# A two-layer hybrid decoder on one Trainium2 core: top-k masks of four blocks as a TensorE product, and two reorderings of conversions

## The chip, the core and the metric

The kernel runs on one core of a Trainium2 chip. Five engines work side by side, each through its own queue in order: TensorE (PE, matrix products), VectorE (DVE), ScalarE (ACT), GpSimd (POOL) and SyncE (SP), which here issues nearly all DMA transfers. An instruction waits until the instructions that it needs on other engines have signalled; everything behind it on its own engine waits with it. The metric is the device time of one launch in microseconds.

## The reference, cut to what matters

The input is one sequence of 1024 tokens of width 1024, in float32. Layer 0 runs sliding-window attention and a state-space branch (S5) with a gated linear unit side by side; layer 1 is sparse attention: an indexer scores all earlier keys for every query, the best 256 are kept, and softmax attention runs over those.

```python
# layer 0, end of the S5 branch
y = jax.nn.gelu(y.reshape(bsz, L, W))
h = y @ glu_w + glu_b
return h[..., :W] * jax.nn.sigmoid(h[..., W:])

# layer 0: both branches side by side, then one projection
return jnp.concatenate([att, ssm], axis=-1) @ w_out

# layer 1, for one block of 128 queries
rel = jax.nn.relu(jnp.einsum('bqhd,bsd->bqhs', qi_blk, ki).astype(jnp.float32) * (IDX_DIM ** -0.5))
score = jnp.einsum('bqhs,bqh->bqs', rel, w_blk.astype(jnp.float32))
score = jnp.where(key_pos[None, None, :] <= t[None, :, None], score, NEG_INF)
_, idx = lax.top_k(score, topk)
...
logits = jnp.einsum('bqhgd,bqkhd->bqhgk', q_blk, k_sel).astype(jnp.float32) * (Dh ** -0.5)
...
logits = jnp.where(valid[:, :, None, None, :], logits + bias, NEG_INF)
p = jax.nn.softmax(logits, axis=-1).astype(v.dtype)
return jnp.einsum('bqhgk,bqkhd->bqhgd', p, v_sel)
```

## The kernel before

Products run in fp32r with each operand split into a high part (rounded) and a low part (the rest), so that each product is three matmuls: high by high, high by low, low by high. A weight chunk comes as `wraw` by DMA; ACT rounds it to `whi` (L153), and DVE or POOL forms `wlo = wraw - whi` (L154). Chunks are numbered in the order of their use; the list `LO_ON_V` (L126) names those whose low part DVE makes, all others go to POOL. Chunks 22 and 23 hold query weights of layer 1, chunk 24 the keys'. A low part is made in four instructions of 128x512.

The order of each engine's instructions comes from a scheduler that follows data dependencies and priorities, except for PE in most stages, where the code writes it out by hand. `behind(insts)` (L128) is a hint of order to that scheduler: what is issued inside it comes after the given instructions.

The linear unit (L852 to L889) runs over two weight chunks `i`, two halves of the tokens and two column groups `n2`, eight rounds in all. In each round PE makes two accumulators of 12 matmuls (L872 to L874); ACT takes a tanh of one (L879), DVE multiplies by the gate (L880) and by the other accumulator (L881), which frees it, and ACT and DVE split the result into high and low (L882, L883), the second half of the tile `cat`. The first half of `cat` is the attention branch: eight loads `at` (L887, four buffers) whose high part ACT makes (L888) and low part DVE (L889). Behind this come the output projections of layer 0, which add the input `xh`, loaded by SP (L903), to PE's product (L911).

In layer 1 the index scores (L1064 to L1072) alternate PE products `psi`, ACT's `relu` (three buffers) and DVE's weighted sum `sc`, while PE also runs the projections of queries, keys and values, whose rows are normalised by way of POOL's `nr` (L199, L200) and ACT's `st` (L392) and then transposed (L1151). The top-k threshold of each block is found by counting in a search: on DVE for blocks 7, 5 and 3 (L1221, which writes a scratch tile `vjunk` beside its counts), on ACT for the others. Ahead of it `flip` (L1198, L1199) turns scores into ordered integers, and after it `tie_mask` (L1282) uses `flip` again and leaves a mask `mk[b]` in bf16 that is zero for a kept key and a large number for another (L1302). Blocks 0 and 1 keep every earlier key; for them `mk0` masks the diagonal block alone.

`dsa_scores` (L1350) does the attention scores of one block and one key head, for four query heads: SP loads the bias tile `bt` (`st` for the first two units), POOL puts the mask on it (L1372 or L1374), PE makes the three score matmuls into `pq` (L1375 to L1377), DVE adds `pq` and `bt` and takes the row's extreme `mn` (L1379), ACT takes the exponential (L1385), and the rows are normalised, on ACT for two heads and on DVE for two (L1390). `dsa_tr` transposes the result on PE (L1401) and splits it (L1404 on ACT, `pT_lo` L1405 on DVE), and `dsa_out` multiplies by the values (L1415 to L1417). The query tile is split by ACT (`q1T_hi`, L1336) and POOL (`q1T_lo`, L1337). The units run blocks 0 to 3 of one key head, blocks 0 to 3 of the other, then blocks 4 to 7; the first two units are scored early, among gate projections, before the masks of the later blocks are ready.

## Time and profile before

| | us |
|---|---|
| median of 3 runs | 1068.32 |
| lowest and highest run | 1062.63, 1068.51 |
| the profiled execution | 1065.89 |
| its span | 1064.2 |

| engine | busy us | share of the span |
|---|---|---|
| PE | 1013.1 | 95% |
| DVE | 748.7 | 70% |
| ACT | 622.3 | 58% |
| POOL | 436.5 | 41% |

The mean granted clock of PE in the profiled execution was 0.987 of full speed. Busy shares are means over stages with different limits; a wait is told by the instruction that waited and the one that came last among those it waited for. In a row of a timeline the last bracket is the idle time ahead of the instruction and what ended it; "x4" means four of the same kind in a row.

### The profile page before, as it was taken

Reading aid. Unit: us, or ns where it says so; the run is one execution under the profiler, and the core shown is the slowest. Engines: PE = TensorE matmul, PEld = TensorE weight load, DVE = VectorE, ACT = ScalarE, POOL = GpSimd, SP = SyncE. Lnnn points to the kernel's source line nnn. Section 1 sums busy time; section 2 is a strip of 40 time slices with the busy share of each in tenths; the row PEclk is TensorE's granted clock in tenths of the full one; section 3 lists DMA queues with packets and bytes.
Section 4 is the critical chain, followed back from the end, with each engine's and each line's share of the span. In section 5 each row is a group of like instructions: output and inputs, shape, how many; then the busy total and the mean of one; then the engine's idle time right before and its main releaser. Section 6 shows DMA issues by size and latency. Waiting matters only on the chain.

```text
span 1064.2 us, 19143 instructions
## 1 busy us (share of the span) xinstructions
PE 1013.1 (95%) x6536; PEld 890.5 (84%) x6536; DVE 748.7 (70%) x1705; ACT 622.3 (58%) x1671; POOL 436.5 (41%) x722
## 2 busy tenths in 40 slices
PE   7899999999998999999999989999998889999998
PEld 5798999999864588877789989999886669898898
DVE  6628889973796554544667578888877986777742
ACT  7543653222787433434566989789967865565620
POOL 5897632221000002122041678678545847456000
PEclk9999999999999999999999999999999989999999
DMA  7282455339462317531020232122436644665333
GB/s 267 95 284 80 105 163 163 107 105 276 133 198 60 100 60 267 207 119 61 1 89 21 75 98 68 41 68 86 121 112 212 204 123 142 201 190 162 117 100 119
DMA packets 103697, 138.33 MB, mean 130 GB/s; under 512 B 9352, under 2 KB 79880, under 8 KB 98736
## 3 DMA queue, kind: packets, MB, share of 16 engines
q1 hardware_dynamic: 103600, 137.12, 41.3%
q8 instruction: 51, 0.84, 0.3%
q14 instruction: 46, 0.38, 0.1%
HBM read 102.31 MB, written 36.21 MB: 130 GB/s over the span
## 4 chain that ended last, share of the span: by engine, by line
PE 68%; DVE 14%; POOL 6%; ACT 5%; DMA 3%; issue 3%; SPq 1%; ACTq 0%; POOLq 0%; DVEq 0%
PE mm L234 8%; PE mm L232 8%; PE mm L233 8%; PE mm L218 5%; PE mm L219 5%; PE mm L220 5%; PE mm L1551 3%; PE mm L1552 3%; PE mm L1550 3%; PE psx L801 2%; PE tr L1401 2%; PE mm L1416 1%; PE mm L1417 1%; PE pq L1375 1%; PE tr L795 1%
## 5 line engine op out<-in xcount | busy, mean ns | idle before, releaser
L153 ACT CAST whi<-wraw 128x512 fp32r<-128x512 f32 (+1 forms) x152 | 87.3, 643 | 74.4 <-PE mm L233 38.2
L154 POOL TENSOR_TENSOR wlo<-wraw,whi 128x512 fp32r<-128x512 f32 x64 | 87.3, 1391 | 96.3 <-ACT whi L153 96.3
L219 PE MATMUL mm<-wlo,h1T_hi 128*128 128x256 f32 x384 | 110.3, 288 | 0.0
L218 PE MATMUL mm<-whi,h1T_hi 128*128 128x256 f32 x384 | 109.8, 288 | 0.2 <-DVE gst L981 0.2
L220 PE MATMUL mm<-whi,h1T_lo 128*128 128x256 f32 x384 | 109.6, 287 | 0.0
L1374 POOL TENSOR_TENSOR bt<-bt,mk 128x384 f32<-128x384 f32 (+3 forms) x80 | 82.5, 1049 | 61.9 <-DMA bt<-g_d 43.9
L919 POOL TENSOR_TENSOR acc<-acc,sq 128x512 f32<-128x512 f32 x12 | 18.1, 1507 | 195.4 <-DVE wlo L154 154.0
L1221 DVE TENSOR_SCALAR_CACHE_REDUCE vjunk<-sc,vt 128x512 bf16<-128x512 uint16 (+5 forms) x90 | 91.0, 1012 | 2.7
L232 PE MATMUL mm<-hT_hi,whi 128*128 128x256 f32 (+1 forms) x288 | 85.6, 297 | 0.0
L234 PE MATMUL mm<-hT_hi,wlo 128*128 128x256 f32 (+1 forms) x288 | 85.6, 297 | 0.0
L233 PE MATMUL mm<-hT_lo,whi 128*128 128x256 f32 (+1 forms) x288 | 85.5, 297 | 0.0
L1257 ACT ACTIVATE sjunk<-sc,st 128x384 bf16<-128x384 uint16 (+5 forms) x90 | 77.7, 864 | 6.2 <-POOL st L1261 4.2
L1550 PE MATMUL mm<-aT_hi,whi 128*128 128x256 f32 x256 | 73.5, 287 | 1.2 <-ACT aT_hi L1524 1.2
L218 PEld LDWEIGHTS mm<-whi,h1T_hi 128*128 128x128 f32 x384 | 72.9, 191 | 1.0 <-PE psi L1065 0.6
L219 PEld LDWEIGHTS mm<-wlo,h1T_hi 128*128 128x128 f32 x384 | 73.2, 191 | 0.4
L154 DVE TENSOR_TENSOR wlo<-wraw,whi 128x512 fp32r<-128x512 f32 (+1 forms) x88 | 62.9, 760 | 15.1 <-ACT whi L153 12.7
L1551 PE MATMUL mm<-aT_lo,whi 128*128 128x256 f32 x256 | 72.7, 284 | 0.7 <-DVE aT_lo L1525 0.7
L220 PEld LDWEIGHTS mm<-whi,h1T_lo 128*128 128x128 f32 x384 | 72.9, 190 | 0.4
L1552 PE MATMUL mm<-aT_hi,wlo 128*128 128x256 f32 x256 | 72.6, 284 | 0.0
L1385 ACT ACTIVATE s<-s,mn 128x384 f32<-128x384 f32 (+7 forms) x56 | 46.0, 821 | 30.9 <-DVE mn L1379 30.9
L1072 DVE SCALAR_TENSOR_TENSOR sc<-relu,wi,sc 128x384 f32<-128x384 f32 (+3 forms) x70 | 49.6, 711 | 20.3 <-ACT relu L1067 16.6
L392 ACT ACTIVATE st<-mm,nr 128x64 f32<-128x64 f32 (+1 forms) x160 | 46.0, 360 | 30.1 <-POOL nr L200 29.9
(398 smaller groups left out, 3478.7 us busy)
## 6 DMA issues: line engine op xcount, KB each, us to landing
wraw<-in_w_dram SPq DMA_DIRECT2D x20, 1024.0 KB, 5.0
wraw<-in_wo_dram SPq DMA_DIRECT2D x16, 1024.0 KB, 5.2
bt<-g_d SPq DMA_DIRECT2D x24, 256.0 KB, 4.6
g_d<-g1r_d SPq DMA_DIRECT2D x8, 576.0 KB, 10.8
bt<-g_d SPq DMA_DIRECT2D x24, 192.0 KB, 3.4
qT_d<-gst SPq DMA_DIRECT2D x32, 128.0 KB, 1.9
qT<-qT_d SPq DMA_DIRECT2D x32, 128.0 KB, 3.9
xh<-in_xT_dram SPq DMA_DIRECT2D x16, 256.0 KB, 5.7
```

The costliest lines, as they stand in the source:

```text
L153: S.copy(hi[p_], raw[p_])
L154: eng.tensor_sub(lo[p_], raw[p_], rd(hi[p_]))
L218: T.matmul(ps, a, hi[:, k, c0:c1], start=(k == 0), stop=False)
L219: T.matmul(ps, a, lo[:, k, c0:c1], start=False, stop=False)
L220: T.matmul(ps, b, hi[:, k, c0:c1], start=False, stop=(k == 7))
L232: T.matmul(o, a, hT[0][:, k, ts], start=(k == 0), stop=False)
L233: T.matmul(o, a, hT[1][:, k, ts], start=False, stop=False)
L234: T.matmul(o, b, hT[0][:, k, ts], start=False, stop=(k == 7))
L1221: V.tensor_scalar(junk[:, :128 * (b + 1)], data(b), self.thr(j), None, op0=OP.is_ge, op1=OP.add, accum_out=self.cnt[:, it, j:j + 1])
L1550: T.matmul(ps, a, aT[0][:, k, toks], start=(k == 0), stop=False)
L1551: T.matmul(ps, a, aT[1][:, k, toks], start=False, stop=False)
L1552: T.matmul(ps, b, aT[0][:, k, toks], start=False, stop=(k == 7))
```

## The change

It has three parts. The linear unit's attention conversions are put behind the last products of a half: those of the first half behind the round that ends chunk 0, those of the second half behind the last round. The low parts of chunks 22 and 23 go from POOL to DVE. And for blocks 0 to 3 POOL no longer puts the mask on the bias tile; PE adds it to the scores itself, as a first bf16 matmul with minus the identity (`nid`) and `mk[b]`, which for blocks 0 and 1 is now a bf16 tile of 256 columns (`mk01`). To make room in SBUF the search's scratch tile `vjunk` shares the memory of `flip`.

```diff
@@ -123,7 +123,7 @@
 
     wcount = [0]
     raw_pools = [wp]
-    LO_ON_V = (0, 1, 2) + tuple(range(9, 21)) + (29, 30) + tuple(range(33, 39))
+    LO_ON_V = (0, 1, 2) + tuple(range(9, 21)) + (22, 23) + (29, 30) + tuple(range(33, 39))
 
     def behind(insts):
 
@@ -853,6 +853,7 @@
         ca = tuple(cps[1 - half].tile([128, 8, 512], F32R, name=f"cat_{n}") for n in ("hi", "lo"))
         cat.append(ca)
     gbt = yp.tile([128, 4, L], F32, name="gbt")
+    glu_last = []
     for n in range(4):
         dma(gbt[:, n], gb_d[n])
     for i in range(2):
@@ -879,14 +880,18 @@
                 S.activation(sg, pp[0], AF.Tanh, scale=0.5, bias=glub[:, 1, 4 + n:5 + n])
                 V.scalar_tensor_tensor(sg, sg, 1.0, gt_, op0=OP.add, op1=OP.mult)
                 V.scalar_tensor_tensor(sg, pp[1], glub[:, 0, n:n + 1], sg, op0=OP.add, op1=OP.mult)
-                S.activation(ca[0][:, 4 + n], sg, AF.Copy, scale=0.25)
-                V.scalar_tensor_tensor(ca[1][:, 4 + n], sg, 0.25, rd(ca[0][:, 4 + n]), op0=OP.mult, op1=OP.subtract)
+                glu_hi = S.activation(ca[0][:, 4 + n], sg, AF.Copy, scale=0.25)
+                glu_lo = V.scalar_tensor_tensor(ca[1][:, 4 + n], sg, 0.25, rd(ca[0][:, 4 + n]), op0=OP.mult,
+                                                op1=OP.subtract)
+            glu_last.append((glu_hi.ins, glu_lo.ins))
     for half in range(2):
         for g in range(4):
             at = st3.tile([128, 512], F32, name="at", bufs=4)
             dma(at, att_d[g, :, half * 512:(half + 1) * 512])
-            S.copy(cat[half][0][:, g], at)
-            V.tensor_sub(cat[half][1][:, g], at, rd(cat[half][0][:, g]))
+
+            with behind(glu_last[1 + 2 * half]):
+                S.copy(cat[half][0][:, g], at)
+                V.tensor_sub(cat[half][1][:, g], at, rd(cat[half][0][:, g]))
     es_y.close()
     es_3.close()
     es_h1 = ExitStack()
@@ -1217,7 +1222,7 @@
             if it % 16 == 0:
                 self.t = self.start()
             for j, b in enumerate(self.blocks):
-                junk = tk.tile([128, L], BF16, name="vjunk")
+                junk = tk.tile([128, L], I32, name="flip").bitcast(BF16)
                 V.tensor_scalar(junk[:, :128 * (b + 1)], data(b), self.thr(j), None, op0=OP.is_ge, op1=OP.add,
                                 accum_out=self.cnt[:, it, j:j + 1])
             i = it % 16
@@ -1317,11 +1322,15 @@
     if "sc7" in dbg:
         dma(dbg["sc7"], sc[7])
 
-    mk0 = mp.tile([128, 128], F32, name="mk0")
+
+    mk01 = mp.tile([128, 256], BF16, name="mk01")
     with tc.issue_after(ki_lo.ins):
-        G.memset(mk0, 0.0)
-    G.affine_select(out=mk0, in_=mk0, pattern=[[-1, 128]], compare_op=OP.is_ge, fill=NEG,
+        G.memset(mk01, 0.0)
+    G.affine_select(out=mk01[:, 128:], in_=mk01[:, 128:], pattern=[[-1, 128]], compare_op=OP.is_ge, fill=FAR,
                     base=0, channel_multiplier=1)
+    mk[0], mk[1] = mk01[:, 128:], mk01
+    nid = mp.tile([128, 128], BF16, name="nid")
+    V.tensor_scalar(nid, ident, -1.0, None, op0=OP.mult)
 
     def dsa_q_load(b, kv):
         qr = akv.tile([128, 4, 128], F32, name="q1r", bufs=2)
@@ -1367,12 +1376,12 @@
                     bp_ = fp if b < 4 and nbt[0] > 6 and nbt[0] % 2 else pool_
                     bt = bp_.tile([128, 512], F32, name="bt", bufs=6)[:, :n]
                 last_ttr[1] = dma(bt, skewed(h, 1023 - 128 * b + c0, n)).ins
-                with behind(last_rstd):
-                    if b < 2:
-                        G.tensor_add(bt[:, w - 128:], bt[:, w - 128:], mk0)
-                    else:
+                if b < 4:
+                    T.matmul(o, nid, mk[b][:, ks], start=True, stop=False)
+                else:
+                    with behind(last_rstd):
                         G.tensor_sub(bt, bt, mk[b][:, ks])
-                T.matmul(o, qT[0][:, g], kT[0][:, kv, ks], start=True, stop=False)
+                T.matmul(o, qT[0][:, g], kT[0][:, kv, ks], start=b > 3, stop=False)
                 T.matmul(o, qT[0][:, g], kT[1][:, kv, ks], start=False, stop=False)
                 T.matmul(o, qT[1][:, g], kT[0][:, kv, ks], start=False, stop=True)
```

The names in the rows that follow are the program's tiles; line numbers of the changed kernel are larger by one to nine (L880 becomes L881, L889 becomes L894, L1072 becomes L1077, L1374 becomes L1383). First DVE at the first rounds of the linear unit, before:

```order
L880 SCALAR_TENSOR_TENSOR sg<-sg,gbt 128x512 x2
L881 SCALAR_TENSOR_TENSOR sg<-mm,glub,sg 128x512
L889 TENSOR_TENSOR cat_lo<-at,cat_hi 128x512 x2
L883 SCALAR_TENSOR_TENSOR cat_lo<-sg,cat_hi 128x512
L889 TENSOR_TENSOR cat_lo<-at,cat_hi 128x512 x3
L881 SCALAR_TENSOR_TENSOR sg<-mm,glub,sg 128x512
L889 TENSOR_TENSOR cat_lo<-at,cat_hi 128x512 x2
```

The same place of DVE in the changed kernel:

```order
L881 SCALAR_TENSOR_TENSOR sg<-sg,gbt 128x512 x2
L882 SCALAR_TENSOR_TENSOR sg<-mm,glub,sg 128x512
L884 SCALAR_TENSOR_TENSOR cat_lo<-sg,cat_hi 128x512
L882 SCALAR_TENSOR_TENSOR sg<-mm,glub,sg 128x512
L884 SCALAR_TENSOR_TENSOR cat_lo<-sg,cat_hi 128x512
L881 SCALAR_TENSOR_TENSOR sg<-sg,gbt 128x512
L882 SCALAR_TENSOR_TENSOR sg<-mm,glub,sg 128x512
L884 SCALAR_TENSOR_TENSOR cat_lo<-sg,cat_hi 128x512
L881 SCALAR_TENSOR_TENSOR sg<-sg,gbt 128x512
L882 SCALAR_TENSOR_TENSOR sg<-mm,glub,sg 128x512
L154 TENSOR_TENSOR wlo<-wraw,whi 128x512 x4
L884 SCALAR_TENSOR_TENSOR cat_lo<-sg,cat_hi 128x512
```

All conversions of attention tiles have left this place; four now stand behind the last row shown and four behind the last round. On SP one weight load of the output projection has moved ahead of the last four loads `at`.

Next DVE in the index scores of block 4 in the changed kernel, where it takes the low part of chunk 22:

```order
L1075 TENSOR_SCALAR sc_5425<-relu,wi 128x320
L1077 SCALAR_TENSOR_TENSOR sc_5425<-relu,wi,sc_5425 128x320
L1058 TENSOR_TENSOR qiT_5429<-mm,qiT_5429 64x512
L1077 SCALAR_TENSOR_TENSOR sc_5425<-relu,wi,sc_5425 128x320 x5
L154 TENSOR_TENSOR wlo<-wraw,whi 128x512 x2
L1077 SCALAR_TENSOR_TENSOR sc_5425<-relu,wi,sc_5425 128x320
L154 TENSOR_TENSOR wlo<-wraw,whi 128x512 x2
L1075 TENSOR_SCALAR sc_5425<-relu,wi 128x320
```

Before, the same rows stand there without the two of L154; those of chunk 23 stand four in a row in the scores of block 6.

Last POOL at the start of the sparse attention, before:

```order
L1372 TENSOR_TENSOR st<-st,mk_9715 128x128 x4
L1337 TENSOR_TENSOR q1T_lo<-q1r,q1T_hi 128x512
L1374 TENSOR_TENSOR bt<-bt,mk_9638 128x384
L1337 TENSOR_TENSOR q1T_lo<-q1r,q1T_hi 128x512
L1374 TENSOR_TENSOR bt<-bt,mk_9638 128x384 x3
L1374 TENSOR_TENSOR bt<-bt,mk_9653 128x512
L1337 TENSOR_TENSOR q1T_lo<-q1r,q1T_hi 128x512
L1374 TENSOR_TENSOR bt<-bt,mk_9653 128x512 x3
L1372 TENSOR_TENSOR bt<-bt,mk_9715 128x128 x3
```

And in the changed kernel, from the same place on:

```order
L1346 TENSOR_TENSOR q1T_lo<-q1r,q1T_hi 128x512 x5
L1383 TENSOR_TENSOR bt<-bt,mk_9668 128x320
L1346 TENSOR_TENSOR q1T_lo<-q1r,q1T_hi 128x512
L1383 TENSOR_TENSOR bt<-bt,mk_9668 128x320
L1346 TENSOR_TENSOR q1T_lo<-q1r,q1T_hi 128x512
```

All mask operations of blocks 0 to 3 are gone from POOL; what is left up to block 4 is the low part of the queries. On PE each group of three score matmuls of these blocks now has a weight load of `nid` and a mask matmul ahead of it; the other rows of PE keep their order in the sparse attention.

## Rows read from the trace of the kernel before

**Rows 1.** Page, part 1: busy us, share of the span, instructions.
```profile
PE 1013.1 (95%) x6536; PEld 890.5 (84%) x6536; DVE 748.7 (70%) x1705; ACT 622.3 (58%) x1671; POOL 436.5 (41%) x722
```

**Rows 2.** Waits of PE, 360 to 370 us: us in total, times, longest.
```profile
PE mm L872 <- DVE sg L881: 2.2, 1, 2.2
```

**Rows 3.** Waits of PE, 530 to 640 us.
```profile
PE tr L1151 <- ACT st L392: 2.9, 1, 2.9
PE psi L1064 <- ACT relu L1067: 0.8, 2, 0.6
```

**Rows 4.** Waits of PE, 811 to 850 us.
```profile
PE tr L1401 <- DVE s L1390: 2.7, 3, 1.7
PE mm L1416 <- DVE pT_lo L1405: 1.9, 3, 1.2
PE pq L1375 <- DVE mn L1379: 1.5, 3, 0.9
PE pq L1375 <- ACT q1T_hi L1336: 1.3, 1, 1.3
```

**Rows 5.** Stretches: us, busy PE, PEld, DVE, ACT, POOL, granted clock, DMA, GB/s.
```profile
820.00:840.00 20.00, 16.73 (x95) 12.70 (x94) 18.75 (x59) 16.52 (x47) 20.00 (x24) 1.00 0.84 273
850.00:862.00 12.00, 10.43 (x54) 9.08 (x54) 10.09 (x35) 9.06 (x18) 4.56 (x6) 0.86 0.57 175
```

**Rows 6.** Timeline of DVE, 355 to 366 us: start, us, instruction, idle before.
```profile
358.73 0.69 DVE L889 TENSOR_TENSOR cat_lo<-at,cat_hi 128x512 fp32r<-128x512 f32 x1 [2.75 <-ACT cat_hi L888]
363.34 0.75 DVE L881 SCALAR_TENSOR_TENSOR sg<-mm,glub,sg 128x512 f32<-128x512 f32 x1
```

**Rows 7.** Timeline of DVE behind the linear unit, 395 to 412 us.
```profile
402.75 0.69 DVE L911 TENSOR_TENSOR xh<-mm,xh 128x512 f32<-128x512 f32 x1 [6.05 <-DMA xh<-in_xT_dram]
405.51 2.49 DVE L154 TENSOR_TENSOR wlo<-wraw,whi 128x512 fp32r<-128x512 f32 x4
```

**Rows 8.** Timeline of PE, 825 to 845 us: neighbours on one accumulator.
```profile
825.53 0.27 PE L1376 MATMUL pq<-k1T_lo,q1T_hi 128*128 128x128 f32 x1
825.64 0.28 PE L1377 MATMUL pq<-k1T_hi,q1T_lo 128*128 128x128 f32 x1
...
840.15 0.34 PE L1375 MATMUL pq<-k1T_hi,q1T_hi 128*128 128x384 f32 x1
840.32 0.34 PE L1376 MATMUL pq<-k1T_lo,q1T_hi 128*128 128x384 f32 x1
...
844.55 0.39 PE L1375 MATMUL pq<-k1T_hi,q1T_hi 128*128 128x512 f32 x1
844.78 0.39 PE L1376 MATMUL pq<-k1T_lo,q1T_hi 128*128 128x512 f32 x1
```

**Rows 9.** Timelines of POOL and DVE, 530 to 620 us.
```profile
545.47 5.77 POOL L154 TENSOR_TENSOR wlo<-wraw,whi 128x512 fp32r<-128x512 f32 x4 [5.40 <-ACT whi L153]
...
548.70 2.89 DVE L1072 SCALAR_TENSOR_TENSOR sc<-relu,wi,sc 128x320 f32<-128x320 f32 x2
...
552.24 1.20 DVE L1072 SCALAR_TENSOR_TENSOR sc<-relu,wi,sc 128x320 f32<-128x320 f32 x2
...
616.84 3.78 POOL L154 TENSOR_TENSOR wlo<-wraw,whi 128x512 fp32r<-128x512 f32 x3
```

**Rows 10.** Page, part 5: busy us, mean ns, idle before.
```profile
L1221 DVE TENSOR_SCALAR_CACHE_REDUCE vjunk<-sc,vt 128x512 bf16<-128x512 uint16 (+5 forms) x90 | 91.0, 1012 | 2.7
```

**Rows 11.** POOL's groups by form, 797 to 841 us: busy us, mean ns, idle before.
```profile
L1374 POOL TENSOR_TENSOR bt<-bt,mk 128x512 f32<-128x512 f32 x8 | 9.4, 1207 | 1.1 <-DMA bt<-g_d 1.1
L1337 POOL TENSOR_TENSOR q1T_lo<-q1r,q1T_hi 128x512 fp32r<-128x512 f32 x6 | 7.8, 1301 | 9.4 <-ACT q1T_hi L1336 9.4
```

**Rows 12.** Timeline of DVE, L1390, 835 to 850 us.
```profile
837.16 1.24 DVE L1390 TENSOR_SCALAR s<-s,den 128x256 f32<-128x256 f32 x1
...
839.10 0.46 DVE L1390 TENSOR_SCALAR s<-s,den 128x256 f32<-128x256 f32 x1
...
848.06 1.35 DVE L1390 TENSOR_SCALAR s<-s,den 128x384 f32<-128x384 f32 x1
```

## The prediction

> **What bounds the kernel now.** I read the page's first part first. TensorE (PE) is busy for 1013.1 of 1064.2 us [rows 1]. So there are about 51 us of PE idle time in the whole run, and a change that takes work off other engines can return only such idle time, or time in which PE runs at half clock. The next view was the waits of PE by stretch, which says who ends each idle time: in the linear unit (around 364 us) one wait of 2.2 us for the `sg` of VectorE (DVE) at L881 [rows 2], in the indexer scores and heads (530 to 640 us) 2.9 us on ACT's `st` and 0.8 us on ACT's `relu` [rows 3], and at the start of the sparse attention (811 to 850 us) several waits, of which those for DVE add up to 6.1 us [rows 4]. Last I read the table by stretch: from 820 to 840 us GpSimd (POOL) is busy for 20.00 of 20 us and DVE for 18.75, while PE has 16.73 [rows 5]. There PE is not the bound. Each of the three edits touches one of these three places.
>
> The sum is made against the profiled execution, 1065.89 us (its span and 1.7 us around it). That execution lies 2.4 us below the median of the three runs and inside their spread of 1062.63 to 1068.51.
>
> **Edit one, the linear unit's conversions.** Before, DVE meets L889 (the low part of an attention tile) ahead of L881 (the product that frees PE's buffer): it stood idle for 2.75 us at 358.73 because ACT's high part was late, did four more of these, and started the second L881 only at 363.34 [rows 6]. In the changed order L881's successor follows one 0.69 us instruction, and ACT's loads from `att_d` no longer stand in front of it. The 2.2 us wait should go. The eight conversions that move cost DVE about 0.6 us each, four in a row 2.5 us, as the same form does at 405.51 [rows 7]. The first four fall between two pairs of GLU products, each pair being 24 matmuls of 512 columns at a pitch of 0.23 us [rows 8], 5.6 us of PE work, so 2.5 us of DVE more stay inside it. The other four fall behind the last GLU product, where DVE stands idle for 6.05 us waiting for `xh` [rows 7]. If that cover were gone they would cost their 2.5 us. On SP's queue a weight load now stands ahead of the last four `at` loads; those wait for the first four buffers to come free and hold up the loads behind them, the `xh` among them, which I cover by the same idle time. Value −2.2 us, bounds −2.2 and 0 (a load becomes late).
>
> **Edit two, low parts of two weights on DVE.** One block of four costs POOL 5.77 us at 545.47. DVE needs about 0.62 us for each of the four, 2.5 us a block and 5.0 for both. But while POOL works on its block, DVE is slow: two L1072 of 128x320 took 2.89 us at 548.70, and two took 1.20 at 552.24 [rows 9]. DVE so gets back about 1.7 us a block, and its net load grows by 0.8 us. PE's waits that lie near these two blocks are the 0.8 us for `relu` [rows 3]. The large wait, 2.9 us at L1151, is of another weight: its chain runs from POOL's `nr` behind the block at 616.84, the key weights (24), which stay on POOL at the same place of its order [rows 9]. So I leave it where it is. Value −0.4 us, half of the 0.8; bounds −0.8, and +5.0 if both blocks are shown to PE in full.
>
> The search's scratch tile shares memory with `flip`, so the first counts of blocks 3 and 5 can't run early; they move behind the last `flip` of the keys. Two counts of 1.0 us in the mean [rows 10] make DVE's search start at most 2 us later. In the stage that follows PE has projections to do and shows no wait of that kind; I count 0, up to +2 if the chain of masks that ends ahead of 811 us is moved by all of it.
>
> **Edit three, the masks as a TensorE product.** POOL loses eight operations of 512 columns between 811 and 841 us (1207 ns each, 9.4 us [rows 11]), eight of 384 and eight of 128 beside them, and eight of 128 in the first two units. PE gains 32 weight loads and 32 matmuls: eight each of 128, 256, 384 and 512 columns. No such bf16 product stands in the trace, so I bound it by the pitch of the fp32r matmuls on the same accumulators: 825.53 to 825.64, 0.11 us for 128 columns; 840.15 to 840.32, 0.17 for 384; 844.55 to 844.78, 0.23 for 512 [rows 8]. With 0.12 to 0.17 for 256 the 32 are 8 x (0.11 + 0.12 + 0.17 + 0.23) = 5.0 us at the low end. The upper bound is the whole duration of such a matmul, not overlapped: 0.27, 0.28, 0.34 and 0.39 us, 10.2 us. I take 5.1, as a weight load of the matmuls here lies beside the matmul before it. By the Trainium skill, TensorE: Matmul & The Clock Gate, section Back-to-back issue gap, the gap is N / 2.4 + 2.5 ns at full clock; by that estimate the 32 would be 4.3 us. No row here has that operation.
>
> Of the 5.1 us, 0.9 (the 128- and 256-column masks of the first two units) fall ahead of 811 us, where PE then waits 1.3 us for ACT's `q1T_hi` [rows 4]; that wait, which hangs on the top-k chain and not on PE, swallows them. So +4.2 us on PE's path behind 811.
>
> What comes back: PE's waits for DVE there are 2.7 us (L1390's normalising), 1.9 (`pT_lo`) and 1.5 (`mn`, the scores' sum) [rows 4]. All three have one source. `mn` waits for POOL's masked `bt`; and L1390 is stretched when POOL works: 128x256 took 1.24 us at 837.16 and 0.46 at 839.10, and one of 128x384 took 1.35 at 848.06 [rows 12], which was the last thing ahead of PE's longest wait in the stretch, 1.7 us. With POOL's work there down to `q1T_lo` (7.8 us for six [rows 11]), I take 5.0 of the 6.1 us as gone. By the Trainium skill, SBUF — State Buffer, section Who interferes with whom, DVE and GpSimd share a port pair as an exclusive lock, so the stretch goes whole and not by half when GpSimd is idle. The rows at 837.16 and 839.10 agree with it; no run here shows it alone.
>
> The wait that ends at 849.46 is followed by a stretch at the lower level: the granted clock of 850 to 862 us is 0.86 [rows 5], (1 − 0.86) x 12 = 1.7 us lost, at 1.2 instead of 2.4 GHz. With the wait mostly gone I take that as gone. Bounds: neither waits nor clock come back (+4.2); all come back and the masks cost their least (4.1 − 6.1 − 1.7 = −3.7). Value 4.2 − 5.0 − 1.7 = −2.5 us.
>
> **Sum.** −2.2 − 0.4 − 2.5 = −5.1 us: 1065.9 − 5.1 = 1060.8, rounded to 1061.
>
> **The rivals.**
> (1) The transfers become the bound at 811 to 850 us. The DMA engines are already busy for 0.84 of 820 to 840 us [rows 5], and POOL waited 1.1 us for a `bt` [rows 11]. Then POOL's queue was only hiding late loads: of the 5.0 us some 1 comes back, the clock falls as before, and edit three gives 4.2 − 1 = +3.2; the total is −2.2 − 0.4 + 3.2 = +0.6, 1066.5. Against it: those 1.1 us are all that POOL waited ahead of its eight operations of 512 columns [rows 11].
> (2) Slower: DVE's two low-part blocks in the scores. `sc` at L1072 frees the buffer that ACT's `relu` and behind it PE's products need. If less than 2.5 us of room is there, PE waits in full, +5.0, and each wait is followed by a clock stretch like the 1.7 us above, +3.4: 1065.9 − 2.2 − 2.5 + 8.4 = 1069.6. It decides from about 2.5 us of wait at a block on. Against it: PE's waits for `relu` were 0.8 us while POOL stretched the same DVE work [rows 3, 9].
> (3) Edit two also mends L1151: with two blocks fewer, POOL comes to `nr` sooner. Then 2.9 us go, and with them a clock stretch, taken at the 1.7 us of the other one: 1060.8 − 4.6 = 1056.2. Against it: the block at 616.84 comes right ahead of that `nr` and hangs on its own weight's conversion.
> (4) The mask products don't overlap and cost 10.2 us: +5.1 less the ones ahead of 811, about +4: 1065.
>
> **How the numbers follow.** Forecast 0.45 (its own range 1058 to 1063.5), rival one 0.2, two 0.1, three 0.13, four 0.12. Both ends are left out at about a tenth each: the range is 1054 (rival three with all waits of edit three gone) to 1068 (rival one with a late search). A measurement here tells about 1% from no change, that is 1057.6 and 1079 against the median of 1068.3. Under 1057.6 lie rival three and the lower edge of the forecast, 0.16; over 1079 nearly nothing, since even rival two stays below: 0.04.
>
> **What would show it.** Right: no wait of over 1 us at the GLU's second product; POOL nearly empty from 811 to 841 apart from `q1T_lo`, L1390 at 128x256 near 0.3 to 0.46 us throughout, no PE wait on it over 0.5 us, PE's busy share from 820 to 840 well over 17 of 20 us. Wrong: PE's waits there named DMA `bt`; waits of over 1 us on `relu` near 548 or 585 us; a mask product with a pitch above 0.3 us; the 2.9 us at L1151 gone.

## The result: 0.84% faster, with more coming from the second part than forecast

The changed kernel took 1057.26 us in the median of four runs (1056.94 to 1058.26), the kernel before 1067.65 us. The ratio is 0.9916, with an interval of 0.989 to 0.9942, so 6 to 12 us; the forecast of 1061 us lay 4 us above the measured time, and its range held it. As a difference the forecast was 5.1 us and this is 9.0 us. Timed again beside other kernels the change gave 0.9929 (0.9907 to 0.995), 7.6 us. It is faster beyond doubt, and by a little less than 1% of the time.

The page's first row for PE after the change, and PE's waits in the three places of the forecast (columns: us in total, times, longest):

```profile
PE 1010.2 (96%) x6568; PEld 888.8 (84%) x6568; DVE 747.0 (71%) x1714; ACT 621.7 (59%) x1671; POOL 399.2 (38%) x682
```

```profile
PE tr L795 <- DVE pT L798: 0.9, 1, 0.9
...
PE psi L1069 <- ACT relu L1072: 0.3, 1, 0.3
...
PE tr L1156 <- ACT st L392: 2.3, 1, 2.3
...
PE pq L1384 <- ACT q1T_hi L1345: 1.4, 1, 1.4
PE mm L1425 <- DVE pT_lo L1414: 1.1, 2, 0.9
PE pq L1384 <- DVE mn L1388: 0.8, 1, 0.8
PE mm L1424 <- ACT pT_hi L1413: 0.6, 1, 0.6
```

At the linear unit none of PE's waits for `sg` is left; the one row there (L795, attention) is the same in both kernels. In the scores 0.8 us for `relu` became 0.3 us, the transpose's 2.9 us became 2.3 us [rows 3]. Between 806 and 846 us the normalising on DVE no longer appears, and the other waits for DVE fell from 3.4 to 1.9 us [rows 4]. PE is 3 us less busy by the page although it has 32 matmuls more: its mean granted clock rose from 0.987 to 0.992.

The stretches that answer to [rows 5] (us, busy PE, PEld, DVE, ACT, POOL, granted clock, DMA share, GB/s), in the kernel after:

```profile
815.00:835.00 20.00, 18.12 (x114) 14.69 (x114) 17.10 (x59) 15.12 (x44) 5.45 (x5) 1.00 0.78 262
845.00:857.00 12.00, 9.78 (x56) 7.50 (x54) 10.22 (x29) 8.64 (x18) 7.30 (x9) 1.00 0.62 194
```

PE is busy for 18.12 of 20 us where it was for 16.73, POOL for 5.45 where it was for 20.00, and the granted clock of the second stretch is 1.00 where it was 0.86.

To put the whole run side by side I took the starts of the same PE instructions in each trace, and took off what PE lost at the lower clock level. The table has the length of each stage at full clock, in us, one profile for each kernel, by the times of the kernel before; the last two columns are the us lost to the lower level between 785 and 880 us, and in the whole run. "Shared" means that the search's scratch tile shares memory with `flip`, as in the full change; part 3 needs that for room.

| kernel | 20 to 357 | 357 to 383, linear unit | 530 to 607, scores | 607 to 640, heads | 785 to 811 | 811 to 850 | 850 to 880 | lost there | lost in all |
|---|---|---|---|---|---|---|---|---|---|
| before | 331.9 | 26.1 | 77.1 | 31.4 | 26.6 | 37.4 | 24.2 | 6.8 | 13.7 |
| full change | 333.6 | 23.0 | 74.9 | 30.9 | 27.4 | 35.0 | 27.0 | 1.7 | 8.5 |
| full, again | 333.9 | 23.0 | 74.8 | 31.1 | 27.4 | 35.2 | 26.6 | 1.7 | 11.9 |
| part 1 | 331.8 | 23.0 | 77.1 | 31.9 | 26.5 | 36.9 | 25.6 | 5.1 | 13.7 |
| part 2 | 333.4 | 25.6 | 75.4 | 34.0 | 27.9 | 35.8 | 26.1 | 3.4 | 10.2 |
| part 3 | 332.2 | 25.7 | 77.1 | 31.4 | 28.3 | 34.1 | 26.2 | 6.8 | 11.9 |
| parts 1, 2 | 334.6 | 23.1 | 75.3 | 32.2 | 27.9 | 37.4 | 24.0 | 8.5 | 15.4 |
| parts 1, 3 | 334.7 | 23.0 | 77.1 | 31.3 | 28.3 | 33.4 | 26.1 | 5.1 | 10.2 |
| parts 2, 3 | 333.2 | 25.3 | 74.9 | 30.9 | 27.4 | 34.9 | 26.7 | 3.4 | 11.9 |
| part 2, shared | 336.9 | 25.8 | 74.9 | 30.7 | 26.8 | 38.2 | 25.4 | 5.1 | 10.2 |
| parts 1, 2, shared | 335.7 | 23.1 | 74.8 | 30.6 | 26.8 | 37.1 | 25.5 | 5.1 | 15.4 |
| POOL kept | 334.2 | 23.0 | 74.9 | 30.5 | 27.4 | 36.4 | 26.7 | 5.1 | 11.9 |
| masks twice | 330.1 | 23.1 | 74.8 | 31.2 | 27.9 | 37.5 | 25.6 | 3.4 | 11.9 |
| full, weight 24 | 333.7 | 23.0 | 74.9 | 28.3 | 32.1 | 34.8 | 26.6 | 10.2 | 13.7 |

The first stage is the same code in every kernel and still scatters from 330.1 to 336.9 us; the loss to the clock scatters from 8.5 to 15.4 us. That is why runs of one kernel lie several us apart, and why the stages tell more than the total. The stretches that no edit touches and that the table leaves out agree: 383 to 530 us takes 146.9 or 147.0 us in every kernel, 640 to 785 us 144.9 to 145.1. Between 588 and 749 us the scheduler orders PE's rows too, and the kernels with part 2 have another order there; the marks at 607 and 640 us are the same products all the same. For the pair of profiles the sum is: first stage +1.7, linear unit −3.1, scores −2.2, heads −0.5 and 1.7 less lost there, 785 to 880 us +1.2 and 5.1 less lost there; behind it −0.8 and 1.7 more lost. That makes −8.8, beside the −8.7 us between the spans 1064.2 and 1055.5.

### The profile page after: what moved, and what is told of

Read it like the earlier page. It is cut to its first block, busy times and chain, and to the rows that moved or that the text cites. A ratio compares the mean times of both kernels' runs of the same rounds, so it can differ in the third digit from the quotient of the medians.

```text
span 1055.5 us, 19157 instructions
## 1 busy us (share of the span) xinstructions
PE 1010.2 (96%) x6568; PEld 888.8 (84%) x6568; DVE 747.0 (71%) x1714; ACT 621.7 (59%) x1671; POOL 399.2 (38%) x682
## 4 chain that ended last, share of the span: by engine, by line
PE 70%; DVE 13%; POOL 5%; DMA 5%; ACT 3%; issue 3%; SPq 1%; POOLq 0%; ACTq 0%; DVEq 0%
PE mm L234 7%; PE mm L232 7%; PE mm L233 7%; PE mm L218 5%; PE mm L219 5%; PE mm L220 5%; PE mm L1560 3%; PE mm L1561 3%; PE mm L1559 3%; PE psx L801 2%; PE tr L1410 2%; PE mm L1425 1%; PE pq L1384 1%; PE pq L1386 1%; PE pq L1385 1%
## 5 line engine op out<-in xcount | busy, mean ns | idle before, releaser
L154 POOL TENSOR_TENSOR wlo<-wraw,whi 128x512 fp32r<-128x512 f32 x56 | 76.3, 1391 | 77.2 <-ACT whi L153 77.2
L1226 DVE TENSOR_SCALAR_CACHE_REDUCE flip<-sc,vt 128x512 bf16<-128x512 uint16 (+5 forms) x90 | 91.0, 1011 | 2.6
L1383 POOL TENSOR_TENSOR bt<-bt,mk 128x320 f32<-128x320 f32 (+3 forms) x64 | 66.4, 1054 | 64.3 <-DMA bt<-g_d 41.7
L154 DVE TENSOR_TENSOR wlo<-wraw,whi 128x512 fp32r<-128x512 f32 (+1 forms) x96 | 64.8, 719 | 13.8 <-ACT whi L153 13.4
L1413 ACT CAST pT_hi<-tr 128x512 fp32r<-128x512 f32 x72 | 41.5, 579 | 37.3 <-PE tr L1410 35.2
L1414 DVE TENSOR_TENSOR pT_lo<-tr,pT_hi 128x512 fp32r<-128x512 f32 x72 | 49.1, 685 | 18.8 <-ACT pT_hi L1413 18.7
```

The source lines that it names most:

```text
L154: eng.tensor_sub(lo[p_], raw[p_], rd(hi[p_]))
L1226: V.tensor_scalar(junk[:, :128 * (b + 1)], data(b), self.thr(j), None, op0=OP.is_ge, op1=OP.add, accum_out=self.cnt[:, it, j:j + 1])
```

## The experiments

**Each part alone.** The first kernel has only the moved conversions.

```diff
+            with behind(glu_last[1 + 2 * half]):
+                S.copy(cat[half][0][:, g], at)
+                V.tensor_sub(cat[half][1][:, g], at, rd(cat[half][0][:, g]))
```

> Only the linear unit's attention conversions are moved; the rest is the kernel before. Theory (the edits act at their own places and add): the two waits of PE at the linear unit, 2.2 and 0.3 us, are gone, and with what stands around them the stretch is 3.1 us shorter, as in the trace of the full change; later work moves with it, so the run is 2.5 to 3.1 us faster (ratio 0.9971 to 0.9977). Rival (the gain of the full change came from clock stretches that fall differently from run to run): the waits go, but the median moves by less than 1 us or by more than 5.

Measured: 0.9959 (0.994 to 0.9978), 4.4 us. The linear unit's stage is 23.0 us, 3.1 shorter; the scores take 77.1 us as before, the heads 31.9 and not 31.4. The theory holds for the stage; the rest of the 4.4 us lies inside the scatter of the other stages. DVE at the place of [rows 6], in the full change (start, us, instruction, idle before):

```profile
356.84 0.75 DVE L882 SCALAR_TENSOR_TENSOR sg<-mm,glub,sg 128x512 f32<-128x512 f32 x1
358.41 0.69 DVE L884 SCALAR_TENSOR_TENSOR cat_lo<-sg,cat_hi 128x512 fp32r<-128x512 f32 x1 [0.83 <-ACT cat_hi L883]
359.02 0.74 DVE L882 SCALAR_TENSOR_TENSOR sg<-mm,glub,sg 128x512 f32<-128x512 f32 x1
```

The second product of the linear unit (L882) starts 2.2 us behind the first, and so it does with part 1 alone (355.69 and 357.86); before it was 8.1 us, from 355.23 to 363.34 [rows 6].

The second kernel has only the two weights.

```diff
-    LO_ON_V = (0, 1, 2) + tuple(range(9, 21)) + (29, 30) + tuple(range(33, 39))
+    LO_ON_V = (0, 1, 2) + tuple(range(9, 21)) + (22, 23) + (29, 30) + tuple(range(33, 39))
```

> Only the low parts of weights 22 and 23 go from GpSimd to VectorE. Theory: PE is 1.2 us earlier behind the place of weight 22 and 0.6 us behind that of weight 23, as in the full change, and the transpose's wait behind weight 24 shrinks from 2.9 to about 2.3 us, without a clock stretch behind it: 2.5 to 4.2 us faster. Rival (the prediction's term): 0.4 us faster, the wait stays at 2.9 us and keeps its clock stretch of 1.7 us, since it hangs on weight 24 alone. Second rival: VectorE's eight more operations are shown to PE, 2 us slower or more.

Measured: 1.0015 (0.9997 to 1.0033), no gain. The scores' stage is 1.7 us shorter, but two other places became longer. PE's waits there, first at the heads, then ahead of the sparse attention:

```profile
PE tr L1151 <- ACT st L392: 4.0, 2, 3.3
...
PE pq L1375 <- DVE mn L1379: 2.1, 1, 2.1
PE pq L1375 <- ACT q1T_hi L1336: 0.5, 1, 0.5
```

The transpose waits for 4.0 us and not 2.9. PE gets a new wait of 2.1 us for the first unit's sum, and in exchange waits 0.5 and not 1.3 us for `q1T_hi` [rows 4]. The second rival had about the size and neither of these places. The chain of the top-k masks grew too. ACT writes one mask after another, blocks 2 to 7; the first and the last of them, in this kernel and then in the full change:

```profile
774.96 0.62 ACT L1302 ACTIVATE mk<-flip,top 128x384 bf16<-128x384 f32 x1
811.40 1.15 ACT L1302 ACTIVATE mk<-flip,top 128x1024 bf16<-128x1024 f32 x1
```

```profile
771.23 0.62 ACT L1307 ACTIVATE mk<-flip,top 128x384 bf16<-128x384 f32 x1 [1.71 <-DVE flip L1302]
804.19 1.15 ACT L1307 ACTIVATE mk<-flip,top 128x1024 bf16<-128x1024 f32 x1 [0.73 <-DVE den L1395]
```

36.4 us lie between them here, 33.0 in the full change (33.1 in the kernel before, 776.39 to 809.53). The query split that the sparse attention waits for stands behind the last mask on ACT. On DVE the scheduler gave this kernel another order of the masks' scans among gate rows and first scores. Of these 3.3 us the table shows 1.3 from 785 to 811 us, and the next stage is 1.6 us shorter; the heads' 2.6 us (31.4 to 34.0) weigh more.

The third kernel has only the masks on TensorE, with the shared tile that makes room for them. The heart of its edit:

```diff
+                if b < 4:
+                    T.matmul(o, nid, mk[b][:, ks], start=True, stop=False)
+                else:
+                    with behind(last_rstd):
```

> Only the masks of blocks 0 to 3 on TensorE, with the shared scratch tile that makes room for them. Theory: PE's waits for VectorE between 811 and 850 us shrink from 6.1 to about 1 us, the masks cost 3.7 us there, and at least one clock stretch goes: 3 to 5 us faster. Rival (transfers bound the stretch): PE waits for masked scores or transfers as long as before and the run is 1 us faster to 1 us slower.

Measured: 0.9991 (0.9973 to 1.001). Neither theory: 811 to 850 us is 3.3 us shorter, as the first said, but 785 to 811 is 1.7 longer and 850 to 880 is 2.0 longer, and as much was lost to the clock as before. The rival's reason isn't there either, since PE's waits named no transfer.

**Pairs, and the full change on the same chip.** The three parts alone sum to −3.8 us, the full change gave twice that.

> The full change once more, beside the next three on one chip. Theory (order of the top-k chain): the three parts don't add, since the chain of masks that ends ahead of the sparse attention sets when PE may go on, and its length hangs on the order that the scheduler gives it: 33 us here, 36 us with the second part alone. So 7 to 10 us faster again (ratio 0.991 to 0.9935). Rival (the parts add): the sum of the three runs, -4.4 + 1.6 - 1.0 = -3.8 us, ratio 0.9964, and the first measurement was scatter.

> The full change without its second part (weights 22 and 23 stay on GpSimd). Both theories: about -5.4 us (ratio 0.995); the chain of masks takes 33 to 34 us. If the theory of the chain holds, the full change is 2 to 4 us faster than this; if the parts add, it is 1.6 us slower than this.

> The full change without its first part (linear unit as before). Theory of the chain: DVE's order in the chain of masks is that of the full change, the chain takes 33 us, and the second part gives its 1.8 to 4 us: 4 to 6 us faster than before (0.9945 to 0.9965). Rival (the parts add): +0.6 us, ratio 1.0005.

> The full change without its third part (masks stay on GpSimd, own scratch tile). DVE's order in the chain of masks is that of the second part alone. Theory of the chain: it takes 36 us again, and PE waits longer ahead of 811 us; -2.5 to -3.5 us (0.9968 to 0.9977), so that the third part is worth 5 to 6 us on top of these two, though it was worth 1.0 alone. Rival (the parts add): -2.8 us as well, but then the full change in this group stands 1.0 us below this one only.

Measured: the full change 0.9929 (0.9907 to 0.995), parts 1 and 3 0.9965 (0.9948 to 0.9981), parts 2 and 3 0.9959 (0.9946 to 0.9972), parts 1 and 2 0.9976 (0.9956 to 0.9996). So the parts don't add in time: the full change is 3.8 us faster than parts 1 and 3, where addition has it 1.6 us slower, and each of the two ratios carries about 2 us either way. With part 3 the second part is worth 2.2 us in the scores (77.1 to 74.9), 0.2 to 0.5 in the heads and 0.9 ahead of 811 us; without it (parts 1, 2 against part 1) the scores give 1.8 but 785 to 811 us takes 1.4 more. The chain of masks took 33.0 us in the full change, 33.2 with parts 2 and 3, and 38.0 with parts 1 and 2. My 5 to 6 us for the third part on top of the first two came out near: 5.0.

The span and the mean granted clock of every timed run are on record, not only of the profiled one. Their product is the run's time at full clock, and the rest of the span is what it lost to the lower level. The means over the runs of each kernel, in us (standard errors 0.2 to 1.1 in the first column, 0.3 to 1.5 in the second):

| kernel (runs) | at full clock | lost to the clock |
|---|---|---|
| before (80) | 1052.9 | 12.0 |
| full change, both timings (10) | 1047.3 | 9.0 |
| part 1 (12) | 1049.4 | 11.6 |
| part 2 (12) | 1051.9 | 14.4 |
| part 3 (12) | 1052.3 | 10.7 |
| parts 1, 2 (12) | 1050.3 | 11.6 |
| parts 1, 3 (6) | 1049.4 | 11.0 |
| parts 2, 3 (11) | 1048.3 | 11.8 |
| part 2, shared (12) | 1050.7 | 12.7 |
| parts 1, 2, shared (10) | 1048.0 | 12.4 |
| POOL kept (6) | 1049.9 | 8.8 |
| masks twice (6) | 1048.3 | 9.3 |
| full, weight 24 (12) | 1049.2 | 13.6 |

At full clock the three parts alone give −3.5, −1.0 and −0.6, in sum −5.1 us, and the full change −5.6: there they do add, within the error. What doesn't add is the loss to the clock: +0.7 us for the three together, −3.0 in the full change, a difference of about two standard errors. The time that my theory of the chain named came; that the chain made it isn't shown.

**What repairs the chain: the shared tile or the masks.** Part 3 brings both. This kernel is the second part with the shared tile alone:

```diff
-                junk = tk.tile([128, L], BF16, name="vjunk")
+                junk = tk.tile([128, L], I32, name="flip").bitcast(BF16)
```

> The second part alone, with the search's scratch tile shared with flip as in the full change, and no mask on TensorE. Theory (the shared tile, which forbids the search's early counts, is what puts the chain of masks and the head rows in a good order): DVE's order in the chain is that of the kernel before, the chain takes 33 to 34 us and not 36, the transpose's wait at the weight 24 block is 2.3 us and not 4.0; 2 to 3 us faster than before (0.997 to 0.998), 3.5 to 4.5 us faster than the second part with its own tile. Rival (the masks on TensorE free GpSimd, and that repairs the chain): 36 us and the time of the second part alone, 1.0015.

Measured: 0.9979 (0.9962 to 0.9996), 3.8 us faster than the second part with its own tile, though this kernel and the next three were timed on another chip, each against the kernel before. PE's wait at the heads and ahead of the sparse attention, and the first and last mask on ACT:

```profile
PE tr L1151 <- ACT st L392: 2.3, 1, 2.3
...
PE pq L1375 <- ACT q1T_hi L1336: 1.5, 1, 1.5
```

```profile
776.32 0.62 ACT L1302 ACTIVATE mk<-flip,top 128x384 bf16<-128x384 f32 x1 [1.71 <-DVE flip L1297]
809.35 1.15 ACT L1302 ACTIVATE mk<-flip,top 128x1024 bf16<-128x1024 f32 x1 [0.42 <-DVE den L1386]
```

2.3 us and not 4.0, no wait for the first unit, and 33.0 us between the masks. So it is the shared tile, and not the masks on PE: it forbids the search's early counts, and the rows of DVE in the chain come, all but one, in the order that they had before. The first count of block 5 with its own tile, and with the shared one:

```profile
571.78 0.95 DVE L1221 TENSOR_SCALAR_CACHE_REDUCE vjunk<-sc 128x768 bf16<-128x768 uint16 x1
...
615.96 0.95 DVE L1221 TENSOR_SCALAR_CACHE_REDUCE flip<-sc 128x768 bf16<-128x768 uint16 x1
```

Where the tile pays is another matter. By the table it is at the heads, 34.0 to 30.7 us, and in the scores, 75.4 to 74.9; in the pair with part 1 it is 32.2 to 30.6 and 75.3 to 74.8. From 785 to 880 us, where the chain ends, the kernels with their own tile take 89.8 and 89.3 us at full clock, those with the shared tile 90.4 and 89.4: a chain of 36.4 or 38.0 us cost PE nothing there. At the heads block 7's `flip` follows block 6's by 23.6 us with the own tile (590.37 to 613.93) and by 22.1 with the shared one (591.16 to 613.24), and POOL's block for weight 24 begins that much later; what in the scheduler's order does it wasn't followed further.

Parts 1 and 2 with the shared tile show what the mask products add to them:

> The full change without the mask products: parts one and two and the shared tile, masks on GpSimd. Theory: parts one and two give 3.1 + 1.9 + 0.7 = 5.7 us, and the mask products add nothing that isn't a clock stretch; so 5 to 6 us faster than before (0.9944 to 0.9953), 1.7 to 3.4 us slower than the full change for one or two clock stretches at the lower level behind 811 us. Rival (the prediction's: waits of PE for DVE are worth more than the masks cost): 3 to 5 us slower than the full change with as many clock stretches.

Measured: 0.9951 (0.993 to 0.9972), as expected; the full change in its two measurements is 2.4 to 3.7 us below it. By the table, at full clock the two are alike from 785 to 880 us: 89.4 us here, 89.4 and 89.2 in the full change. The difference there is 5.1 against 1.7 us lost to the clock. The timed runs say the same: 1048.0 and 1047.3 us at full clock, 12.4 and 9.0 us lost.

**What POOL's work cost.** POOL does the subtractions again, into a tile that nobody reads, while PE's masks are used.

```diff
+                    if pool_ is not gp:
+                        pj = fp.tile([128, 512], F32, name="pj", bufs=1)[:, :n]
+                        with behind(last_rstd):
+                            G.tensor_sub(pj, bt, mk[b][:, ks])
```

> The full change, but GpSimd still does the subtractions of masks of blocks 0 to 3 behind the first two units, into a scratch tile that nobody reads; TensorE's masks are the ones used. Theory (the waits were GpSimd's contention with DVE's normalising, and its work standing ahead of q1T_lo): L1390 on DVE stretches again to over 1 us, PE's waits between 811 and 850 us come back to over 4 us, and the run is 3 to 5 us slower than the full change. Rival (the wait of the sum for the masked bias tile was the matter, which is gone here): PE waits 2 us or less there, the run is within 1.5 us of the full change.

Measured: 0.994 (0.9918 to 0.9962), 1.2 us behind the full change timed with the pairs, which is less than the two ratios can tell apart, so nearer the rival. The group of DVE's normalising with 384 columns between the same places, in the kernel before, here, and in the full change (columns: busy us, mean ns):

```profile
L1390 DVE TENSOR_SCALAR s<-s,den 128x384 f32<-128x384 f32 x4 | 4.1, 1047 | 0.0
...
L1403 DVE TENSOR_SCALAR s<-s,den 128x384 f32<-128x384 f32 x4 | 3.0, 742 | 0.0
...
L1399 DVE TENSOR_SCALAR s<-s,den 128x384 f32<-128x384 f32 x4 | 1.8, 450 | 0.0
```

1047, 742 and 450 ns: about half of the stretch comes back with POOL's work, and 811 to 850 us takes 36.4 us where the full change has 35.0 and 35.2. PE's waits don't come back as I had expected:

```profile
PE mm L1429 <- DVE pT_lo L1418: 1.4, 3, 0.6
PE mm L1428 <- ACT pT_hi L1417: 1.2, 1, 1.2
PE pq L1380 <- DVE mn L1392: 0.4, 1, 0.4
```

By that stage, one profile each, POOL's work beside DVE is worth about 1.3 us, the smaller share of the waits of [rows 4]. The larger would be that the sum and what follows it no longer wait for POOL; this is what is left over, and no run shows it alone.

**The price of the mask products.** Each is issued twice.

```diff
                     T.matmul(o, nid, mk[b][:, ks], start=True, stop=False)
+                    T.matmul(o, nid, mk[b][:, ks], start=False, stop=False)
```

> The full change with every mask product issued twice (a masked score gets twice the large number, the result is the same). The price of the 32 products alone: with the pitches in the trace of the full change, 0.05, 0.11, 0.17 and 0.23 us for 128, 256, 384 and 512 columns, 4.5 us, of which 3.3 to 4.2 us show behind 811 us. Theory (PE is the bound there once GpSimd is out): 3 to 4.5 us slower than the full change. Rival (DVE and ACT still set the pace there): the products fill waits, less than 1.5 us slower.

Measured: 0.9931 (0.9908 to 0.9954), which alone doesn't tell it from the full change. By the stages the second set costs 0.5 us ahead of 811 and 2.4 us from 811 to 850, and 1.0 to 1.4 come back from 850 to 880: 1.5 to 1.9 of its 4.5 us show. The rest went into waits:

```profile
PE pq L1385 <- ACT q1T_hi L1345: 1.0, 1, 1.0
PE mm L1426 <- DVE pT_lo L1415: 0.4, 1, 0.4
PE mm L1425 <- ACT pT_hi L1414: 0.3, 1, 0.3
```

The products' own pitch stands in the full change (timeline of PE, one group of 512 columns from mask to mask):

```profile
812.52 0.39 PE L1380 MATMUL pq<-mk,nid 128*128 128x512 bf16 x1
812.56 0.58 PE L1384 MATMUL pq<-k1T_hi,q1T_hi 128*128 128x512 f32 x1
812.98 0.39 PE L1385 MATMUL pq<-k1T_lo,q1T_hi 128*128 128x512 f32 x1
813.20 0.40 PE L1386 MATMUL pq<-k1T_hi,q1T_lo 128*128 128x512 f32 x1
813.44 0.39 PE L1380 MATMUL pq<-mk,nid 128*128 128x512 bf16 x1
```

0.92 us for four matmuls, 0.23 each; three at the pitch of [rows 8] take 0.69. The mask is recorded as starting only 0.04 us ahead of the next matmul, which then has the longer pitch. By the same count 384 columns cost 0.17, 256 cost 0.11 and 128 cost 0.05 us: 4.5 us for all 32.

**A third weight on DVE.** This is the full change with weight 24 moved as well, the one whose block stands ahead of the transpose's wait.

```diff
-(22, 23) + (29, 30)
+(22, 23, 24) + (29, 30)
```

> The full change, and the low part of weight 24 (keys) on VectorE too. Theory: the wait of 2.3 us at the head transpose is GpSimd's block for weight 24 standing ahead of the row norms; it falls under 0.5 us, and the run is 1.5 to 2.3 us faster than the full change, 10 to 12 us under the kernel before (ratio 0.988 to 0.991). Rival: the norms are late for ScalarE's sake (it makes weight 24's high part in four casts ahead of them), the wait stays over 1.5 us and the time is that of the full change, 0.9916.

Measured: 0.9979 (0.9962 to 0.9996), 5 to 7 us slower than the full change. The wait at the heads did go, and the stage is 2.7 us shorter; PE came 4.7 us earlier to the place of 784 us than in the first profile of the full change. But the time was given back ahead of the sparse attention. PE's waits from 600 to 812 us:

```profile
PE pq L1384 <- ACT q1T_hi L1345: 5.1, 1, 5.1
PE pq L1380 <- DVE mn L1388: 2.7, 2, 2.4
```

The chain of masks took 40.8 us (first to last mask on ACT):

```profile
768.71 0.62 ACT L1307 ACTIVATE mk<-flip,top 128x384 bf16<-128x384 f32 x1 [1.78 <-DVE flip L1302]
809.54 1.15 ACT L1307 ACTIVATE mk<-flip,top 128x1024 bf16<-128x1024 f32 x1 [0.65 <-DVE flip L1302]
```

Here the scheduler put two of the masks' scans behind the first units' scores on DVE. From 785 to 880 us this kernel takes 93.5 us at full clock, 4 us more than the full change, and it loses 10.2 us to the clock there. The theory of the wait was right, and what I expected of the time wrong: at this length the chain and not PE sets when the sparse attention starts.

## Why the prediction came out

**The sum.** By all timed runs the change is worth 5.6 us at full clock and 3.0 us less lost to the lower level (standard errors 0.6 and 1.0). I had 3.4 and 1.7 us. The three places and the direction were right; the size came out too small, and the time fell into the range because that was 14 us wide. Rival three's time, 1056.2, lay nearer to the measured 1057.3 us than the forecast did, though its mechanism held for 0.6 of its 2.9 us only.

**Part 1, right in mechanism, the term too small.** The wait of 2.2 us went, and nothing took its place at the eight moved conversions. I had left the 0.3 us for ACT's `sg` standing behind it; it went as well, and so did the slower matmuls that follow a wait: the first one behind the 2.2 us has its successor 0.33 us later (364.14 to 364.47), where the pitch is 0.23. The stage takes 23.0 or 23.1 us in every kernel with the part, and 25.3 to 26.1 in the five without it: −2.2 was up to 0.9 us short.

**Part 2, the term mis-sized.** I had −0.4 us and measured −2.2 in the scores and −0.5 in the heads. The step that failed is the one from [rows 3] to the value: I took half of the listed waits as what can come back. But a listed wait is less than what PE loses by it. Before, around the longer of the two:

```profile
551.32 0.27 PE L1000 MATMUL mm<-h1T_hi,wlo 128*128 128x256 f32 x1
552.18 0.44 PE L1064 MATMUL psi<-kiT,qiT 128*128 128x384 f32 x1 [0.59 <-ACT relu L1067]
552.46 0.34 PE L1065 MATMUL psi<-kiT,qiT 128*128 128x384 f32 x1
```

The pitch of the first row's kind is 0.12 us, and that of the last two 0.17 (553.64 to 553.82). PE so stands 0.74 us where 0.59 are listed, and the next pair starts 0.28 apart: 0.85 us in all. The wait of 0.2 us goes the same way, and a third, of 0.2 us for DVE's `gst` (L981) at 587.52, which stands outside [rows 3], goes too. What made them is as I had it: DVE's sums beside POOL's blocks. The group of 320 columns from 530 to 611 us, before, and in the full change (busy us, mean ns):

```profile
L1072 DVE SCALAR_TENSOR_TENSOR sc<-relu,wi,sc 128x320 f32<-128x320 f32 x14 | 9.8, 701 | 1.5 <-ACT relu L1067 0.5
...
L1077 DVE SCALAR_TENSOR_TENSOR sc<-relu,wi,sc 128x320 f32<-128x320 f32 x14 | 7.7, 550 | 1.0
```

DVE got back 2.1 us there; I had 1.7 for a block. At the heads I said that the 2.9 us hang on weight 24 alone; they do hang on it, for the wait disappears when that weight moves, but the two blocks fewer took 0.6 us off it, and in the profile of the full change no clock loss followed it. In other profiles with 2.3 us one did, so that 1.7 us is not the part's.

**The shared tile, not weighed.** I gave it 0 to +2 us as a delay of the search. Without it the second part is 3.8 us slower, and the first two parts 2.7 us (0.9976 and 0.9951); each of these carries about 3 us either way, and at full clock the timed runs give 1.2 and 2.3 us. Rival two, the slower case, didn't come: PE's waits for `relu` didn't grow. But the second part alone gained nothing, by a way that I hadn't named, the order of rows at the heads.

**Part 3, the value near, and partly by luck.** Of 6.1 us of PE's waits for DVE I took 5.0 as gone and 4.2 us as the price of the masks behind 811: −0.8 at full clock, and −1.7 for the clock. Four pairs of kernels differ by the masks on PE, the first two also by the shared tile: part 3 and before, parts 1, 3 and part 1, parts 2, 3 and part 2 with the tile, the full change and parts 1, 2 with the tile. Their timed runs differ by −0.6, 0.0, −2.4 and −0.7 us at full clock, −0.9 in the mean, and by −1.3, −0.6, −0.9 and −3.4 us lost to the clock, −1.6 in the mean (standard errors 0.4 and 0.5).

But the −0.8 is the sum of stages that I had otherwise. Over the kernels with and without the part, 811 to 850 us is 2.6 us shorter (34.5 against 37.1, means of five and six), for the masks cost less there (the doubled ones add 2.4 us). The 0.9 us ahead of 811 were not swallowed: in the four pairs that stage is longer by 0.6 to 1.8 us. And 850 to 880 us is 1.4 us longer: PE comes to block 4 earlier, and its waits there for DVE and ACT are 6.3 us in the full change, where they were 4.9.

My reading of [rows 12] was wrong in two points. The 0.46 us at 839.10 isn't a row with POOL idle, and the 1.35 us at 848.06, ahead of the wait of 1.7 us that I took as gone, didn't stand beside a mask. POOL at these places:

```profile
835.94 4.28 POOL L1374 TENSOR_TENSOR bt<-bt,mk 128x512 f32<-128x512 f32 x4
...
847.92 1.26 POOL L1337 TENSOR_TENSOR q1T_lo<-q1r,q1T_hi 128x512 fp32r<-128x512 f32 x1 [1.07 <-ACT q1T_hi L1336]
```

POOL works through 839.10 without a gap, and at 848.06 it makes `q1T_lo`, which the change keeps. PE's wait for the normalising went all the same.

The clock stretch that I named, behind that wait, stands in three of the six profiles without the masks on PE (before, parts 1 and 2, part 2 with the tile), and in none of the eight that have them. So it did go with the part, but half of the kernels without the part don't have it either; −1.7 us for one profile is about half of that in the mean. Other stretches make up the rest, and the profiles differ too much among themselves (1.7 to 6.8 us lost from 785 to 880 with the part) to tell which; why parts 1 and 3 and part 3 alone kept more isn't shown.

**The rivals.** Transfers as the bound fell: no PE wait from 806 to 846 us names one. Masks that don't overlap fell: 4.5 us and not 10.2. By the Trainium skill, TensorE: Matmul & The Clock Gate, section Back-to-back issue gap, the sum had been estimated at 4.3 us from the formula for an isolated matmul; the trace agrees better with it, by 4.5, than with my 5.1 from the fp32r neighbours. By the Trainium skill, SBUF — State Buffer, section Who interferes with whom, DVE and GpSimd share a port pair that one of them holds exclusively. The 1047 ns that fell to 450 and rose to 742 with POOL's work agree with it, and so does a row of 512 columns that still took 1.26 us at 842.59 in the full change, beside POOL's `q1T_lo` of 842.26 to 843.57, where the next of that form took 0.47 (846.80).

## What to carry to other kernels

Look for the chain that sets when a stage may start, and measure its length before and after, even when no edit touches it: here 33 us became 36 to 41 us because a scheduler reordered rows around it. Then look whether the stages pay for it: at 36 and 38 us they didn't, at 41 us a gain of 2.7 us ahead of it was worth nothing. Time an edit by the stage that it touches, from one PE instruction to the same one in the other trace and at one clock level, since the unchanged first stage of this kernel scatters by more than any one edit is worth, and where every run has its granted clock on record, split the times of all of them by it. When parts are tried alone, keep what they share (here a scratch tile that only made room): here it was worth 2.7 and 3.8 us in two pairs.

## What the runs showed of the hardware that I had not expected

A wait of the same length is sometimes followed by a stretch at 1.2 GHz and sometimes not. The 2.3 us at the heads was followed by one in the full change timed again and by none in its first profile, and the 1.4 and 0.8 us ahead of the sparse attention by none in both of them and by one with parts 2 and 3. Each cost about 1.7 us. The profiles lost 8.5 to 15.4 us to them in all, the timed runs 3 to 20 us.

In the full change a bf16 matmul ahead of fp32r ones shows its time in the record of the matmul behind it: the mask of 512 columns starts at 812.52, the next matmul at 812.56, and the one after that at 812.98, 0.42 us later. Read alone, the mask's row would tell a pitch of 0.04 us; only the group of four does tell its price.
